# Two-layer hybrid decoder trunk: three merge columns' retention and GLA parts placed between the S5 gate blocks

## Chip, cores and metric

The kernel runs on one core of one Trainium2 chip. The metric is the device time of one execution in microseconds; the median of three runs is 2176.14 us (2175.97 to 2176.38).

## The reference

A sequence of 272 tokens (16 meta tokens and 256 others) of width 2048 passes through two layers, each a single mixer with a residual. On the same normalised input three token mixers run side by side: retention with 8 heads, gated linear attention (GLA) with 4 heads, and a diagonal complex state space model (S5) of 64 groups. Their outputs are merged column by column under sigmoid gates.

```python
h = rmsnorm(h_res, norm_g)
proj = h @ w_in
(rq, rk, rv, rg, gq, gk, gv, gg, glr, su, sg, mg) = jnp.split(proj, offs, axis=-1)
...
ro = (ro * jax.nn.silu(rg.astype(f32))).astype(dt)
...
go = (go.reshape(bsz, length, BRANCH_WIDTH) * jax.nn.silu(gg.astype(f32))).astype(dt)
...
so = jax.nn.gelu(so)
so = so * jax.nn.sigmoid(so @ s5_w_glu.astype(f32))
so = (so * jax.nn.silu(sg.astype(f32))).astype(dt)
g_r, g_g, g_s = jnp.split(mg, N_BRANCH, axis=-1)
y = (jax.nn.sigmoid(g_r) * (ro @ w_br_ret)
     + jax.nn.sigmoid(g_g) * (go @ w_br_gla)
     + jax.nn.sigmoid(g_s) * (so @ w_br_s5))
return h_res + y @ w_out
```

After the second layer a last RMSNorm follows and the meta tokens are dropped. All is float32.

## The kernel before

Activations lie transposed: 128 channels on the partitions, the 272 tokens along the free axis (256 of them in most of layer 1, where `c0` is 16). The unit of work is a block (`block`, line 180): 128 output columns of one weight matrix. It takes the weights in half blocks of eight 128x128 pieces. `prefetch` (line 128) loads each half block from memory through SyncE's queue, splits it into a rounded high part on ScalarE (ACT, line 137) and the remainder on VectorE (DVE, line 139), with three buffers for each. PE multiplies high by high, high by low and low by high. Where twice the token count fits 512 columns (layer 1, for the blocks called with `wide`), the two products with the high weights are one matmul of 512 columns (line 191), joined afterwards by a copy on ACT and an addition on DVE (lines 201 and 202); otherwise there are three matmuls a piece (lines 194 to 196).

`schedule` (line 66) is the order of all blocks of a layer, and the weights lie in memory in that order (`layout`). In order: GLA heads 0 and 1, eight S5 input blocks `su`, GLA heads 2 and 3, eight retention heads (`rv`, `rk`, `rq`, `rg`), eight S5 gate blocks `sg`, eight blocks `glu`, sixteen merge columns, sixteen output blocks. A merge column is six blocks: a sigmoid gate from the input and a projection of a branch's result, for retention (`mr`, `br`), GLA (`mgg`, `bg`) and S5 (`ms`, `bs`). The gate blocks have two half blocks, the projections one.

The S5 recurrence is a scan over 136 pairs of tokens (`s5_scan`, line 538), three instructions on GpSimd (POOL) for a step, all on the one tile `H`. It begins after the last `su` block and runs on POOL beside the GLA and retention heads. When it has ended, `s5_out(b)` (line 551) computes the eight S5 outputs: on PE one matmul of line 554, which does not read `H`, and eight of line 557, which do; on DVE nine short instructions (lines 561 to 569); on ACT a GELU. `so_split` then makes high and low parts for `glu`, which reads all eight outputs in each of its blocks.

Small pieces of work that depend on a block are put off by `after(n, fn)` (line 148): `fn` is emitted when `n` more half blocks have been emitted. `bg_finish(scan)` emits the rest of the scan. Before, it and the outputs hang on retention gate block 6:

```python
                if i == RH - 2:
                    after(6, partial(bg_finish, scan))
                    for b in range(NB):
                        after(6 + 3 * b // 2, partial(s5_out, b))
```

So output 0 follows the last block of `rq` of head 7, with that head's gate block and the eight `sg` blocks behind it. A scheduler then fixes each engine's order of instructions ahead of the run, and each engine works through its own in that order. Work tiles of 128x288 come from a pool of 17 (`U`), small PSUM tiles from a pool of five (`PT`), blocks' accumulators from three.

Of the kernel before, what the change touches and what calls it, by code (L numbers as in the profile page):

```python
# [17 lines left out]
ALU = mybir.AluOpType  # L18
# [13 lines left out]
NB = BW // P  # L32
RH = 8
# [2 lines left out]
GROUPS = 64  # L36
PAIRS = 32
HALF = T // 2

OFF = {}  # L40
_o = 0
# [24 lines left out]
def schedule():  # L66

    o = []

    def gla(h):  # L70
        o.extend([("gv", 2 * h, 16), ("gv", 2 * h + 1, 16), ("gk", h, 16), ("gq", h, 16), ("gg", 2 * h, 16),
                  ("gg", 2 * h + 1, 16)])

    gla(0)
    gla(1)
    o.extend(("su", b, 16) for b in range(NB))
    gla(2)
    gla(3)
    for h in range(RH):
        o.extend([("rv", h, 16), ("rk", h, 16), ("rq", h, 16), ("rg", h, 16)])  # L80
    o.extend(("sg", b, 16) for b in range(NB))
    o.extend(("glu", b, 8) for b in range(NB))
    for d in range(KT):
        o.extend([("mr", d, 16), ("br", d, 8), ("mgg", d, 16), ("bg", d, 8), ("ms", d, 16), ("bs", d, 8)])
    o.extend(("out", d, 16) for d in range(KT))
    return o

# [2 lines left out]
def hybrid(ctx: ExitStack, tc: tile.TileContext, xT, wst, wg, small, bcp, cst, rot, dec, out):  # L90
# [53 lines left out]
    bg = deque()  # L144
# [183 lines left out]
    for l in range(DEPTH):  # L328
# [432 lines left out]
            return h  # L761

        mg = {}
        for kind, i, nk in schedule():
            if kind == "gv":
                if i == 0:
                    after(3, partial(gla_tables, 0))
                if i % 2 == 0:
                    gl = {}
                vt = ev_v(block(x, nk, 0))  # L770
                after(1, partial(tokens, vt, False, gl, f"v{i % 2}"))
            elif kind == "gk":
                ev_gk(block(x, nk, 0), i, gl)
            elif kind == "gq":
                ev_gq(block(x, nk, c0), i, gl)
                after(1, partial(gla_scores, i, gl))
                after(3, partial(gla_apply, gl))
                after(5, partial(gla_norm, gl))
            elif kind == "gg":
                z = gate(block(x, nk, c0))  # L780
                after(7 - 3 * (i % 2), partial(lambda z, gl, i: gated(z, gl["n"][i % 2], s1, i), z, gl, i))
                if i % 2 == 0 and i < 6:
                    gla_tables(i // 2 + 1)
            elif kind == "su":
                if i == 0:
                    bg_finish(prep)
                    s5["H"] = tp.tile([P, 2, PAIRS, HALF], F32, tag="big", name=nm("H"))
                ps = block(x, nk, 0)
                V.tensor_tensor(out=su[:, i], in0=ps.rearrange("p (n e) -> p e n", e=2),  # L789
                                in1=R.rearrange("p (n e) -> p e n", e=2), op=ALU.mult)  # L790
                u2 = U().rearrange("p (a b) -> p a b", a=2)
                for v_ in range(2):
                    for pr in range(2):
                        for e in range(2):
                            G.dma_start(out=u2[64 * pr + 32 * e:64 * pr + 32 * e + 32, v_, :],  # L795
                                        in_=su[64 * v_ + 32 * pr:64 * v_ + 32 * pr + 32, i, e, :])
                after(2, partial(s5_weights, i))
                after(5, partial(s5_in, i, u2))
                if i == NB - 1:
                    scan = s5_scan()  # L800
                    after(6, partial(bg.append, scan))
            elif kind == "rv":
                if i == 0:
                    s2 = tp.tile([P, 2, NB, T], F32R, tag="s2", name=nm("ro"))
                    rot_tables()
                rl = {}
                vt = ev_v(block(x, nk, 0))
                after(1, partial(tokens, vt, True, rl, "v"))
            elif kind == "rk":
                rl["k"] = rope(block(x, nk, 0), 0)  # L810
            elif kind == "rq":
                rl["q"] = rope(block(x, nk, c0), c0)
                after(1, partial(ret_scores, i, rl))
                after(3, partial(ret_apply, rl))
                after(5, partial(ret_norm, i, rl))
            elif kind == "rg":
                z = gate(block(x, nk, c0))
                after(5, partial(lambda z, rl, i: gated(z, rl["n"], s2, i), z, rl, i))
                if i == RH - 2:
                    after(6, partial(bg_finish, scan))  # L820
                    for b in range(NB):
                        after(6 + 3 * b // 2, partial(s5_out, b))
            elif kind == "sg":
                if i == 0:
                    sgs = []
                ps = block(x, nk, c0, True)
                z = U()
                V.tensor_tensor(out=z[:, c0:], in0=ps, in1=R[:, c0:], op=ALU.mult)  # L828
                S.activation(z[:, c0:], z[:, c0:], AF.Silu)
                sgs.append(z)  # L830
                if i == 4:
                    s5["so"] = tp.tile([P, 2, NB, T], F32R, tag="big", name=nm("sohl"))
                if i >= 4:
                    for b in (2 * i - 8, 2 * i - 7):
                        so_split(b)
                        so = su[:, b, :, n0:]
                        G.tensor_tensor(out=so, in0=so, in1=sgs[b][:, c0:].rearrange("p (n e) -> p e n", e=2),
                                        op=ALU.mult)
            elif kind == "glu":
                if i == 0:  # L840
                    s3 = tp.tile([P, 2, NB, T], F32R, tag="s3", name=nm("so2"))
                z = sig(block(s5["so"], nk, c0, True), False)
                t = U()
                G.tensor_tensor(out=t[:, c0:].rearrange("p (n e) -> p e n", e=2), in0=su[:, i, :, n0:],  # L844
                                in1=z[:, c0:].rearrange("p (n e) -> p e n", e=2), op=ALU.mult)
                split(s3[:, 0, i, c0:], s3[:, 1, i, c0:], t[:, c0:])
            elif kind in ("mr", "mgg", "ms"):
                if kind == "mr" and i == 0:
                    y = tp.tile([P, 2, KT, T], F32R, tag="big", name=nm("y"))
                mg["s"] = sig(block(x, nk, c0, True))  # L850
            elif kind in ("br", "bg", "bs"):
                mv = {"br": s2, "bg": s1, "bs": s3}[kind]
                ps = block(mv, nk, c0, True)
                t = mg["s"]
                V.tensor_tensor(out=t[:, c0:], in0=ps, in1=t[:, c0:], op=ALU.mult)  # L855
                if kind == "br":
                    mg["y"] = t
                elif kind == "bg":
                    G.tensor_tensor(out=t[:, c0:], in0=t[:, c0:], in1=mg["y"][:, c0:], op=ALU.add)  # L859
                    mg["y"] = t  # L860
                else:
                    V.tensor_tensor(out=t[:, c0:], in0=t[:, c0:], in1=mg["y"][:, c0:], op=ALU.add)
                    split(y[:, 0, i, c0:], y[:, 1, i, c0:], t[:, c0:])
            elif kind == "out":
                if i == 0:
                    acc = []
                    tc.keep_in_program_order(S.preload_act_table_set("natural_log_exp_and_others"))
                    hn_next = load_h(0)
                    if last:
                        hf = tp.tile([P, KT, 256], F32, tag="s1", name=nm("hf"))  # L870
                    else:
                        xn = new_x()
                        gps, gmm = rank_gate(l + 1, xn)
                hold = hn_next
                if i < KT - 1:
                    hn_next = load_h(i + 1)
                ps = block(y, nk, c0, i < KT - 1)
                if not last:
                    h = U()
                    V.tensor_tensor(out=h, in0=ps, in1=hold, op=ALU.add)  # L880
                    split(xn[:, 0, i, :], xn[:, 1, i, :], h, sm(l + 1, "ng", i))
                    accumulate(h, acc)
                    gmm(i)
                    G.dma_start(out=h1[i], in_=h)
                else:
                    h = hf[:, i, :]
                    V.tensor_tensor(out=h, in0=ps, in1=hold[:, c0:], op=ALU.add)  # L887
                    accumulate(h, acc, c0)
                    S.activation(h, h, AF.Copy, scale=sm(l, "fg", i))
# [96 lines left out]
```

## Time and profile before

| quantity | value |
|---|---|
| median of three runs | 2176.14 us |
| the profiled execution | 2176.12 us |
| its span, first to last instruction | 2174.3 us |
| PE busy, matmuls | 2101.0 us (97%) |
| DVE / ACT / POOL busy | 1445.0 / 1022.8 / 754.1 us |
| mean granted clock of PE | 0.985 |
| loads of weight half blocks | 656 of 512 KB |

Busy time is the time in which an engine works on an instruction. PE's matmuls overlap, so a busy PE is not PE at its peak. The time of the whole is set by what ends last: where PE has work all along, a shorter time can come only from places in which it rests or runs at a lower clock. The views that are read below are the page, the list of waits (which engine and line waited for which), the timeline (instructions in order of time), the groups of instructions by line, and stretches of the span with the busy time of each engine.

### The profile page before, as it was taken

Reading aid. Unit: us, or ns where it says so; the run is one execution under the profiler, and the core shown is the slowest. Engines: PE = TensorE matmul, PEld = TensorE weight load, DVE = VectorE, ACT = ScalarE, POOL = GpSimd, SP = SyncE. Lnnn points to the kernel's source line nnn. Section 1 sums busy time; section 2 is a strip of 40 time slices with the busy share of each in tenths; the row PEclk is TensorE's granted clock in tenths of the full one; section 3 lists DMA queues with packets and bytes.
Section 4 is the critical chain, followed back from the end, with each engine's and each line's share of the span. In section 5 each row is a group of like instructions: output and inputs, shape, how many; then the busy total and the mean of one; then the engine's idle time right before and its main releaser. Section 6 shows DMA issues by size and latency. Waiting matters only on the chain. (4 is left out here: it accounts for less than half of the span.)

```text
span 2174.3 us, 39777 instructions
## 1 busy us (share of the span) xinstructions
PE 2101.0 (97%) x15650; PEld 1996.6 (92%) x15650; DVE 1445.0 (66%) x2370; ACT 1022.8 (47%) x1516; POOL 754.1 (35%) x1111
## 2 busy tenths in 40 slices
PE   9999999959999999999999999999499999999997
PEld 8999999959999999999999999999488888888886
DVE  7955888858555555555668648888496666666655
ACT  6655433326434434444446554444165444444554
POOL 3164888871200000002321548888803000000022
PEclk9999999979999999999999999999799999999999
DMA  6454444423545555445664444445235555555564
GB/s 228 137 166 137 163 161 161 161 90 125 177 175 175 175 175 175 175 175 194 210 205 147 162 141 161 168 165 172 90 107 184 194 185 192 186 190 188 189 214 152
DMA packets 108412, 365.47 MB, mean 168 GB/s; under 512 B 14016, under 2 KB 21696, under 8 KB 107968
## 3 DMA queue, kind: packets, MB, share of 16 engines
q1 hardware_dynamic: 101536, 353.73, 47.4%
q0 software_dynamic: 6400, 8.92, 1.3%
q8 instruction: 123, 2.02, 0.4%
q14 instruction: 65, 0.53, 0.1%
q10 hardware_dynamic: 288, 0.27, 0.0%
HBM read 356.32 MB, written 4.33 MB: 166 GB/s over the span
## 5 line engine op out<-in xcount | busy, mean ns | idle before, releaser
L137 ACT ACTIVATE hi<-raw 128x1024 fp32r<-128x1024 f32 x656 | 694.7, 1059 | 969.6 <-PE acc L195 574.9
L139 DVE TENSOR_TENSOR lo<-raw,hi 128x1024 fp32r<-128x1024 f32 x656 | 825.9, 1259 | 426.9 <-ACT hi L137 423.3
L196 PE MATMUL acc<-x,lo 128*128 128x272 f32 (+1 forms) x3840 | 1103.9, 288 | 2.1 <-DVE lo L139 2.1
L194 PE MATMUL acc<-x,hi 128*128 128x272 f32 (+1 forms) x2944 | 857.1, 291 | 1.1 <-ACT hi L137 0.9
L195 PE MATMUL acc<-x,hi 128*128 128x272 f32 (+1 forms) x2944 | 850.1, 289 | 0.0
L196 PEld LDWEIGHTS acc<-x,lo 128*128 128x128 f32 x3840 | 725.0, 189 | 3.8 <-DVE lo L139 3.0
L194 PEld LDWEIGHTS acc<-x,hi 128*128 128x128 f32 x2944 | 556.2, 189 | 8.0 <-issue 3.9
L195 PEld LDWEIGHTS acc<-x,hi 128*128 128x128 f32 x2944 | 556.5, 189 | 0.9
L191 PE MATMUL acc<-x,hi 128*128 128x512 f32 x896 | 317.8, 395 | 1.4 <-DVE u L828 1.2
L859 POOL TENSOR_TENSOR u<-u,u 128x272 f32<-128x272 f32 (+1 forms) x32 | 24.2, 757 | 768.1 <-DVE u L855 743.7
L542 POOL TENSOR_TENSOR pr<-H,tab 128x128 f32<-128x128 f32 x270 | 208.3, 771 | 70.9 <-ACT H L536 49.9
L191 PEld LDWEIGHTS acc<-x,hi 128*128 128x128 f32 x896 | 168.9, 189 | 41.1 <-ACT su L571 1.7
L544 POOL TENSOR_TENSOR H<-H,pr 128x64 f32<-128x64 f32 x270 | 162.2, 601 | 21.2
L545 POOL TENSOR_TENSOR H<-H,pr 128x64 f32<-128x64 f32 x270 | 143.3, 531 | 21.2
L196 PE MATMUL acc<-y,lo 128*128 128x272 f32 (+1 forms) x512 | 145.7, 285 | 0.0
L196 PEld LDWEIGHTS acc<-y,lo 128*128 128x128 f32 x512 | 96.3, 188 | 0.4
L191 PE MATMUL acc<-y,hi 128*128 128x512 f32 x240 | 83.8, 393 | 0.0
L194 PE MATMUL acc<-y,hi 128*128 128x272 f32 (+1 forms) x272 | 78.4, 288 | 0.0
L195 PE MATMUL acc<-y,hi 128*128 128x272 f32 (+1 forms) x272 | 78.2, 288 | 0.0
L795 POOL DMA_DIRECT2D u<-su x128 | 63.1, 501 | 39.2 <-DVE su L789 18.5
L196 PE MATMUL acc<-so,lo 128*128 128x272 f32 (+1 forms) x256 | 72.9, 285 | 0.0
L196 PE MATMUL acc<-ro,lo 128*128 128x272 f32 (+1 forms) x256 | 72.9, 285 | 0.0
(285 smaller groups left out, 2664.8 us busy)
## 6 DMA issues: line engine op xcount, KB each, us to landing
raw<-wst SPq DMA_DIRECT2D x656, 512.0 KB, 3.3
h<-xT SPq DMA_DIRECT2D x8, 272.0 KB, 5.6
u<-su POOLq DMA_DIRECT2D x128, 17.0 KB, 2.8
u<-dec SPq DMA_DIRECT2D x16, 136.0 KB, 3.3
u<-xT POOLq DMA_DIRECT2D x16, 136.0 KB, 2.5
h<-u POOLq DMA_DIRECT2D x16, 136.0 KB, 2.4
u<-h POOLq DMA_DIRECT2D x16, 136.0 KB, 4.2
pre<-bcp SPq DMA_DIRECT2D x2, 1024.0 KB, 8.0
```

The source lines that it names most:

```text
L137: S.activation(hi, raw, AF.Copy)
L139: V.tensor_tensor(out=lo, in0=raw, in1=hi.bitcast(F32), op=ALU.subtract)
L191: PE.matmul(ps[:, 0:2 * w].rearrange("p (j t) -> p j t", j=2), hi[:, k, :], mv[:, :, kk, c0:T], start=(kk == 0), stop=False, skip_group_ch ...
L194: PE.matmul(o, hi[:, k, :], mv[:, 0, kk, c0:T], start=(kk == 0), stop=False)
L195: PE.matmul(o, hi[:, k, :], mv[:, 1, kk, c0:T], start=False, stop=False)
L196: PE.matmul(o, lo[:, k, :], mv[:, 0, kk, c0:T], start=False, stop=(kk == nk - 1), skip_group_check=both)
L542: G.tensor_tensor(out=pr, in0=H[:, :, :, n - 1].unsqueeze(1).broadcast_to([P, 2, 2, PAIRS]), in1=tab.rearrange("p (k r) q -> p k r q", k=2 ...
L544: G.tensor_tensor(out=H[:, :, :, n], in0=H[:, :, :, n], in1=pr[:, 0], op=ALU.add)
L545: G.tensor_tensor(out=H[:, :, :, n], in0=H[:, :, :, n], in1=pr[:, 1, ::-1, :], op=ALU.add)
L795: G.dma_start(out=u2[64 * pr + 32 * e:64 * pr + 32 * e + 32, v_, :], in_=su[64 * v_ + 32 * pr:64 * v_ + 32 * pr + 32, i, e, :])
L859: G.tensor_tensor(out=t[:, c0:], in0=t[:, c0:], in1=mg["y"][:, c0:], op=ALU.add)
```

## The change

The first four `sg` blocks come, then the retention and GLA parts of merge columns 0 to 2 (`mr`, `br`, `mgg`, `bg`), then the other four `sg` blocks and `glu`. In the merge stage behind `glu`, columns 0 to 2 have only their S5 part (`ms`, `bs`) left. The end of the scan and the S5 outputs hang no longer on retention gate block 6 but on `mr` of column 1, three half blocks on. The sums of the three columns are kept, each in a work tile of its own, until `bs`; their addition of the retention and GLA parts is made by DVE, the other columns' by POOL as before. The tile `y` is allocated at the first `ms`.

```diff
@@ -36,6 +36,7 @@
 GROUPS = 64
 PAIRS = 32
 HALF = T // 2
+AHEAD_D = 3
 
 OFF = {}
 _o = 0
@@ -78,10 +79,15 @@
     gla(3)
     for h in range(RH):
         o.extend([("rv", h, 16), ("rk", h, 16), ("rq", h, 16), ("rg", h, 16)])
-    o.extend(("sg", b, 16) for b in range(NB))
+    o.extend(("sg", b, 16) for b in range(4))
+    for d in range(AHEAD_D):
+        o.extend([("mr", d, 16), ("br", d, 8), ("mgg", d, 16), ("bg", d, 8)])
+    o.extend(("sg", b, 16) for b in range(4, NB))
     o.extend(("glu", b, 8) for b in range(NB))
     for d in range(KT):
-        o.extend([("mr", d, 16), ("br", d, 8), ("mgg", d, 16), ("bg", d, 8), ("ms", d, 16), ("bs", d, 8)])
+        if d >= AHEAD_D:
+            o.extend([("mr", d, 16), ("br", d, 8), ("mgg", d, 16), ("bg", d, 8)])
+        o.extend([("ms", d, 16), ("bs", d, 8)])
     o.extend(("out", d, 16) for d in range(KT))
     return o
 
@@ -761,6 +767,7 @@
             return h
 
         mg = {}
+        s3 = None
         for kind, i, nk in schedule():
             if kind == "gv":
                 if i == 0:
@@ -816,10 +823,6 @@
             elif kind == "rg":
                 z = gate(block(x, nk, c0))
                 after(5, partial(lambda z, rl, i: gated(z, rl["n"], s2, i), z, rl, i))
-                if i == RH - 2:
-                    after(6, partial(bg_finish, scan))
-                    for b in range(NB):
-                        after(6 + 3 * b // 2, partial(s5_out, b))
             elif kind == "sg":
                 if i == 0:
                     sgs = []
@@ -845,7 +848,11 @@
                                 in1=z[:, c0:].rearrange("p (n e) -> p e n", e=2), op=ALU.mult)
                 split(s3[:, 0, i, c0:], s3[:, 1, i, c0:], t[:, c0:])
             elif kind in ("mr", "mgg", "ms"):
-                if kind == "mr" and i == 0:
+                if kind == "mr" and i == AHEAD_D - 2:
+                    after(3, partial(bg_finish, scan))
+                    for b in range(NB):
+                        after(3 + 3 * b // 2, partial(s5_out, b))
+                if kind == "ms" and i == 0:
                     y = tp.tile([P, 2, KT, T], F32R, tag="big", name=nm("y"))
                 mg["s"] = sig(block(x, nk, c0, True))
             elif kind in ("br", "bg", "bs"):
@@ -854,12 +861,13 @@
                 t = mg["s"]
                 V.tensor_tensor(out=t[:, c0:], in0=ps, in1=t[:, c0:], op=ALU.mult)
                 if kind == "br":
-                    mg["y"] = t
+                    mg[i] = t
                 elif kind == "bg":
-                    G.tensor_tensor(out=t[:, c0:], in0=t[:, c0:], in1=mg["y"][:, c0:], op=ALU.add)
-                    mg["y"] = t
+                    e = V if i < AHEAD_D else G
+                    e.tensor_tensor(out=t[:, c0:], in0=t[:, c0:], in1=mg[i][:, c0:], op=ALU.add)
+                    mg[i] = t
                 else:
-                    V.tensor_tensor(out=t[:, c0:], in0=t[:, c0:], in1=mg["y"][:, c0:], op=ALU.add)
+                    V.tensor_tensor(out=t[:, c0:], in0=t[:, c0:], in1=mg.pop(i)[:, c0:], op=ALU.add)
                     split(y[:, 0, i, c0:], y[:, 1, i, c0:], t[:, c0:])
             elif kind == "out":
                 if i == 0:
```

On PE in layer 1, where output 0 stood behind the last piece of `rq` of head 7 (`acc_18788`); `yp` is the output's PSUM tile, `K` and `C` tables of the S5 part, `su` its input. Before:

```order
L194 MATMUL acc_18788<-x_11840,hi_18754 128x256
L195 MATMUL acc_18788<-x_11840,hi_18754 128x256
L196 MATMUL acc_18788<-x_11840,lo_18756 128x256
L554 MATMUL yp_18852<-su_13031,K_1035_14157 128x128
L557 MATMUL yp_18852<-H_14166,C_13901 64x129 x8
L194 MATMUL acc_18878<-x_11840,hi_18791 128x256
L195 MATMUL acc_18878<-x_11840,hi_18791 128x256
L196 MATMUL acc_18878<-x_11840,lo_18793 128x256
```

In the change the matmuls on `H` of output 0 stand behind the last piece of `br` of column 1, which reads retention's result `ro`:

```order
L197 MATMUL acc_19374<-ro_16021,hi_19326 128x512
L202 MATMUL acc_19374<-ro_16021,lo_19328 128x256
L197 MATMUL acc_19374<-ro_16021,hi_19326 128x512
L202 MATMUL acc_19374<-ro_16021,lo_19328 128x256
L197 MATMUL acc_19374<-ro_16021,hi_19326 128x512
L202 MATMUL acc_19374<-ro_16021,lo_19328 128x256
L563 MATMUL yp_19397<-H_14166,C_13901 64x129 x8
L197 MATMUL acc_19421<-x_11840,hi_19348 128x512
L202 MATMUL acc_19421<-x_11840,lo_19350 128x256
```

Between the two places are 320 matmuls of blocks, and its first matmul, on `su`, stands among the `sg` blocks. In layer 0 the same move spans 456.

On DVE in layer 1, one S5 output (lines 561 to 569) between two weight remainders `lo`. Before, output 2, beside retention head 7 (`ur` is a part of its norm):

```order
L139 TENSOR_TENSOR lo_19028<-raw_19024,hi_19026 128x1024
L561 SCALAR_TENSOR_TENSOR su_13031<-su_13031,sm_73,yp_18994 128x128
L566 SCALAR_TENSOR_TENSOR su_13031<-su_13031,sm_73,yp_18994 32x128
L569 TENSOR_TENSOR su_13031<-su_13031,yp_18994 32x128
L566 SCALAR_TENSOR_TENSOR su_13031<-su_13031,sm_73,yp_18994 32x128
L569 TENSOR_TENSOR su_13031<-su_13031,yp_18994 32x128
L566 SCALAR_TENSOR_TENSOR su_13031<-su_13031,sm_73,yp_18994 32x128
L569 TENSOR_TENSOR su_13031<-su_13031,yp_18994 32x128
L566 SCALAR_TENSOR_TENSOR su_13031<-su_13031,sm_73,yp_18994 32x128
L569 TENSOR_TENSOR su_13031<-su_13031,yp_18994 32x128
L208 TENSOR_TENSOR ur_19021<-u_19018,ur_19020 128x256
L139 TENSOR_TENSOR lo_19077<-raw_19073,hi_19075 128x1024
```

In the change, output 1 (the same lines are 567 to 575, and 139 is 145):

```order
L145 TENSOR_TENSOR lo_19468<-raw_19464,hi_19466 128x1024
L567 SCALAR_TENSOR_TENSOR su_13031<-su_13031,sm_73,yp_19444 128x128
L572 SCALAR_TENSOR_TENSOR su_13031<-su_13031,sm_73,yp_19444 32x128
L575 TENSOR_TENSOR su_13031<-su_13031,yp_19444 32x128
L572 SCALAR_TENSOR_TENSOR su_13031<-su_13031,sm_73,yp_19444 32x128
L575 TENSOR_TENSOR su_13031<-su_13031,yp_19444 32x128
L572 SCALAR_TENSOR_TENSOR su_13031<-su_13031,sm_73,yp_19444 32x128
L575 TENSOR_TENSOR su_13031<-su_13031,yp_19444 32x128
L572 SCALAR_TENSOR_TENSOR su_13031<-su_13031,sm_73,yp_19444 32x128
L575 TENSOR_TENSOR su_13031<-su_13031,yp_19444 32x128
L145 TENSOR_TENSOR lo_19497<-raw_19493,hi_19495 128x1024
L208 TENSOR_TENSOR acc_19421<-acc_19421,u_19486 128x256
```

The S5 outputs moved from the stretch of head 7 and the gate blocks to that of merge columns 1 and 2.

On DVE at the end of `glu` in layer 1 (`so` is the result of a `glu` block). Before, after the last `glu` block's part the gate of `mr`, column 0:

```order
L139 TENSOR_TENSOR lo_19840<-raw_19836,hi_19838 128x1024
L208 TENSOR_TENSOR so_1634_19555<-u_19808,so_1634_19555 128x256
L139 TENSOR_TENSOR lo_19869<-raw_19865,hi_19867 128x1024
L202 TENSOR_TENSOR acc_19813<-acc_19813,u_19858 128x256
L752 TENSOR_TENSOR u_19861<-acc_19813,R_13015 128x256
L139 TENSOR_TENSOR lo_19896<-raw_19892,hi_19894 128x1024
L202 TENSOR_TENSOR acc_19864<-acc_19864,u_19887 128x256
L855 TENSOR_TENSOR u_19861<-acc_19864,u_19861 128x256
```

In the change its successor is the gate of `ms` (line 758), and then the product of `bs` (line 862) and the sum with the kept tile (line 870):

```order
L145 TENSOR_TENSOR lo_20311<-raw_20307,hi_20309 128x1024
L214 TENSOR_TENSOR so_1664_20026<-u_20279,so_1664_20026 128x256
L145 TENSOR_TENSOR lo_20340<-raw_20336,hi_20338 128x1024
L208 TENSOR_TENSOR acc_20284<-acc_20284,u_20329 128x256
L758 TENSOR_TENSOR u_20332<-acc_20284,R_13015 128x256
L145 TENSOR_TENSOR lo_20370<-raw_20366,hi_20368 128x1024
L208 TENSOR_TENSOR acc_20335<-acc_20335,u_20358 128x256
L145 TENSOR_TENSOR lo_20392<-raw_20388,hi_20390 128x1024
L862 TENSOR_TENSOR u_20332<-acc_20335,u_20332 128x256
L870 TENSOR_TENSOR u_20332<-u_20332,u_19292 128x256
```

`mr`, `br`, `mgg` and `bg` of column 0 stood between the last `glu` block and `ms`, and stand there no more.

## Rows read from the trace of the kernel before

**Rows 1.** Profile page: busy time by engine, and PE's busy tenths in 40 slices.

```profile
PE 2101.0 (97%) x15650; PEld 1996.6 (92%) x15650; DVE 1445.0 (66%) x2370; ACT 1022.8 (47%) x1516; POOL 754.1 (35%) x1111
...
PE   9999999959999999999999999999499999999997
```

**Rows 2.** PE's waits, whole span: us in total, times, longest.

```profile
PE yp L557 <- POOL H L545: 51.0, 2, 28.3
...
PE acc L196 <- DVE lo L139: 2.1, 3, 0.9
```

**Rows 3.** PE's timeline around S5 output 0: start us, us, instruction [idle before <-releaser].

```profile
479.46 2.08 PE L557 MATMUL yp<-H,C 128*64 128x136 f32 x16 [22.76 <-POOL H L545]
...
1573.11 1.99 PE L557 MATMUL yp<-H,C 128*64 128x129 f32 x16 [28.29 <-POOL H L545]
...
1578.83 0.38 PE L554 MATMUL yp<-su,K 128*128 128x128 f32 x2
...
1580.17 0.39 PE L194 MATMUL acc<-x,hi 128*128 128x256 f32 x1
```

**Rows 4.** Stretches of PE: us, busy (matmuls), granted clock, DMA share, GB/s.

```profile
479.40:485.00 5.60, 5.54 (x32) 0.52 0.01 3
...
1573.10:1577.00 3.90, 3.89 (x25) 0.50 0.00 0
...
1625.40:1631.50 6.10, 3.95 (x14) 0.73 0.35 99
```

**Rows 5.** POOL's timeline, scan steps that remain when PE reaches S5 output 0.

```profile
455.58 1.37 POOL L542 TENSOR_TENSOR pr<-H,tab 128x128 f32<-128x128 f32 x1
...
478.03 0.51 POOL L542 TENSOR_TENSOR pr<-H,tab 128x128 f32<-128x128 f32 x1
...
1545.91 0.51 POOL L542 TENSOR_TENSOR pr<-H,tab 128x128 f32<-128x128 f32 x1
...
1571.69 0.51 POOL L542 TENSOR_TENSOR pr<-H,tab 128x128 f32<-128x128 f32 x1
```

**Rows 6.** POOL's groups, 200 to 450, then 1300 to 1540 us: count | busy.

```profile
L542 POOL TENSOR_TENSOR pr<-H,tab 128x128 f32<-128x128 f32 x113 | 89.0, 788 | 8.9
...
L542 POOL TENSOR_TENSOR pr<-H,tab 128x128 f32<-128x128 f32 x107 | 88.5, 827 | 8.4
```

**Rows 7.** Stretches, all engines: PE, weight loads, DVE, ACT, POOL, clock, DMA, GB/s.

```profile
550.00:950.00 400.00, 400.00 (x3174) 400.00 (x3173) 214.94 (x250) 165.17 (x205) 23.41 (x23) 1.00 0.50 175
...
1700.00:2050.00 350.00, 350.00 (x2006) 307.04 (x2005) 228.76 (x322) 172.23 (x264) 10.38 (x14) 1.00 0.55 189
```

**Rows 8.** DVE's groups from 1570 to 1660 us.

```profile
L139 DVE TENSOR_TENSOR lo<-raw,hi 128x1024 fp32r<-128x1024 f32 x22 | 27.4, 1247 | 12.7 <-ACT hi L137 12.5 <-ACT u L201 0.2
...
L566 DVE SCALAR_TENSOR_TENSOR su<-su,sm,yp 32x128 f32<-32x128 f32 x32 | 10.9, 340 | 0.3
L569 DVE TENSOR_TENSOR su<-su,yp 32x128 f32<-32x128 f32 x32 | 9.2, 287 | 0.5
L202 DVE TENSOR_TENSOR acc<-acc,u 128x256 f32<-128x256 f32 x12 | 5.1, 423 | 0.8 <-ACT u L201 0.7
```

**Rows 9.** PE's timeline near the end of the gate blocks, layer 1.

```profile
1626.67 0.47 PE L191 MATMUL acc<-x,hi 128*128 128x512 f32 x1 [1.25 <-DVE u L828]
...
1628.04 0.45 PE L196 MATMUL acc<-x,lo 128*128 128x256 f32 x1 [0.91 <-DVE lo L139]
```

**Rows 10.** Timeline, end of glu, layers 0 and 1: last matmul, last subtractions.

```profile
576.02 0.29 PE L196 MATMUL acc<-sohl,lo 128*128 128x272 f32 x1
...
582.48 0.44 DVE L208 TENSOR_TENSOR so<-u,so 128x272 fp32r<-128x272 f32 x1 [1.14 <-ACT so L207]
...
1666.86 0.28 PE L196 MATMUL acc<-sohl,lo 128*128 128x256 f32 x1
...
1672.64 0.42 DVE L208 TENSOR_TENSOR so<-u,so 128x256 fp32r<-128x256 f32 x1 [0.75 <-ACT so L207]
...
1675.90 0.43 DVE L208 TENSOR_TENSOR so<-u,so 128x256 fp32r<-128x256 f32 x1 [1.09 <-ACT so L207]
```

## Prediction, on record before the change was run

> **What bounds the kernel now.** The page comes first. TensorE (PE) is busy for 2101.0 of 2174.3 us, and among the forty slices its row falls to 5 and 4 at two inner places, one in each layer [rows 1]. So the whole is PE's stream of matmuls, and only what interrupts that stream can be won. PE's list of waits says what does: 51.0 us in two waits of line 557 for POOL, against 2.1 us for the next largest entry [rows 2]. The timeline shows both: before the matmuls of S5 output 0 that read the scan's tile (line 557), PE stands for 22.76 us in layer 0 and 28.29 us in layer 1 until POOL's last scan addition [rows 3]. After such a rest the granted clock is 0.52 of full for 5.6 us and 0.50 for 3.9 us, the lower of PE's two levels (1.2 of 2.4 GHz) for nearly all of it [rows 4]. POOL is not idle in these waits. It does the remaining scan steps (three instructions each, the first on line 542): 15 starts from 455.58 to 478.03, and 18 starts from 1545.91 to 1571.69 [rows 5]. The scan is simply not finished when PE's queue reaches the S5 outputs, and everything behind in that queue waits with them.
>
> The profiled execution took 2176.12 us, 0.02 under the median of the three runs, so the sum is made from 2176.1. Some 0.2% (4.4 us) is what a measurement of this kernel can tell from no change.
>
> **The change, part by part.**
>
> *The S5 outputs move back by 19 half blocks.* Between the old and the new place of output 0 stand 456 matmuls in layer 0 (152 on each of three lines) and 320 in layer 1: 48 single ones of the last retention gate and 136 pairs. Single matmuls of 272 columns run at 400/3174 = 0.126 us each, the pairs at 350/2006 = 0.1745 per matmul [rows 7]; for 256 columns I scale the first to 0.1185. The cover is 456 x 0.126 = 57.5 us in layer 0 and 48 x 0.1185 + 272 x 0.1745 = 53.2 us in layer 1; the twelve small attention matmuls between them are left out, on the safe side. All of this is independent of the scan.
>
> *The scan is slower when PE no longer rests.* While PE and VectorE (DVE) work, a scan step takes 250/113 = 2.21 us in layer 0 and 240/107 = 2.24 us in layer 1 (instances of line 542 in those stretches, [rows 6]); in the wait, with little on DVE, the starts are 25.8/17 = 1.52 us apart, the first of them still disturbed [rows 5]. So the remainder must be counted at the slow pace: 15 x 2.21 = 33.2 us against 57.5, and 18 x 2.24 = 40.3 us against 53.2. Both waits go, with margins of 24 and 13 us. The Trainium skill, "SBUF — State Buffer", section "Who interferes with whom", says why: a DVE instruction with two SBUF inputs holds the port that GpSimd reads through, exclusively, for its whole length. By that rule alone, with the weight subtraction of line 139 (1.25 us of each 2.79 us half block), POOL keeps 55% of the time, the 27.4 us of scan left in layer 1 at the undisturbed pace would need 50 us, and the wait would be gone by a margin of 3 only, which DVE's other instructions with two SBUF inputs could use up: by the rule the second rival below, by the rows the sum as it stands. What I use is the rows' 40.3. The bound above, worked out from rows: if POOL moved only while DVE is idle, 35% of the time in the merge stage (228.76 of 350 busy, [rows 7]), it would do 0.35 x 53.2 = 18.6 of the 18 x 1.52 = 27.4 us, and PE would rest for 8.8 us. Below, the wait is zero. I take zero, since the rows of 250 and 240 us are the same contention.
>
> *Gain of this part:* 22.76 + 28.29 of rest, and the slow clock behind it, 5.6 x 0.48 + 3.9 x 0.50 = 2.7 + 1.95. Together **55.7 us**.
>
> *The load on DVE after the first S5 output.* An S5 output costs DVE 4 x 340 + 4 x 287 ns and a ninth instruction that I take like the first four, 2.85 us [rows 8]. Before, all eight fell, after the rest, together with the finishing of retention head 7, and DVE was the late one at the end: PE waited 1.25 us for a gate's evacuation and 0.91 us for a weight remainder [rows 9], and the clock fell again. In the 6.1 us from 1625.4 only 14 matmuls began [rows 4], worth 14 x 0.1745 = 2.4, so 3.7 us were lost. In the change head 7 is finished before output 0, and the outputs lie two to every three half blocks. In layer 1 such three cost DVE 3 x 1.247 (line 139) + 2 x 0.42 (line 202) + 0.85 (lines 752 and 855, of line 202's size) + 0.2 (half an addition, which the change gives to DVE) + 2 x 2.85 = 11.35 us, and PE 48 x 0.1745 + 2 x 1.34 = 11.05 us (1.34 is 1580.17 less 1578.83, [rows 3]). DVE is behind by 0.3 us per three, four times: 1.2 us. After that come gate blocks, where DVE has room. In layer 0 the three take PE 72 x 0.126 + 2.7 = 11.8 us and DVE, without the two joins, about 10.6: nothing. So I take the old loss of 3.7 as gone and 1.2 as new. The bounds are 0, since hi and lo have three buffers each to absorb it, and 3.7, the old stall once more.
>
> *What costs nothing.* The six additions that go from POOL (line 859) to DVE are in the sum above; on POOL they would have stood behind the scan. ScalarE gets four table loads fewer (50 for 54) and is 47% busy [rows 1]. SyncE issues the same loads in the new order, and only one decay table changes its place among them; DMA was busy for half of that time [rows 7]. The first matmul of output 0 is issued early in layer 1 and holds one of five PSUM buffers.
>
> *Behind glu the cover shrinks.* Before, eight half blocks stood between glu block 7 and the first use of its result in `bs`, now the two of `ms`. The chain behind glu (ACT, POOL, ACT, DVE) runs at its own pace of 1675.90 - 1672.64 = 3.26 us a block, slower than PE. In layer 1 its last subtraction ended at 1676.33, 9.2 us after PE's last glu matmul at 1667.14; in layer 0 at 582.92, 6.6 us after 576.31 [rows 10]. The last of the eight operands is wanted after two half blocks and seven eighths of a third: 16 x 2.875 x 0.1745 = 8.0 us in layer 1, 24 x 2.875 x 0.126 = 8.7 us in layer 0. So layer 1 pays 9.2 - 8.0 = 1.2 us, layer 0 nothing. Bounds: 0, if the chain runs a little ahead, and 9.2 - 5.6 = 3.6 us with some 2 us of slow clock, if `bs` has to wait with its first operand for the last one.
>
> **Sum:** 2176.1 - 55.7 - 3.7 + 1.2 + 1.2 = **2119.1**, say 2119 us, 2.6% faster.
>
> **Rivals.**
>
> *DVE becomes the bound.* The S5 outputs now share DVE with merge columns, which are its heaviest stage beside the heads. For it: 11.35 against 11.05 us, where any disorder in the queue delays a weight remainder, and a delayed remainder stops PE and lowers its clock, as [rows 9] show. Against it: the excess is small, and it is preceded by an unloaded stretch. If the old stall comes back in both layers, 2119 + 2 x 3.7 = 2126.4 us.
>
> *The scan is still late in layer 1.* For it: DVE's work slows POOL (1.52 to 2.24 us a step), and the merge columns bring DVE work of their own. Against it: the 2.24 us were themselves measured beside a working DVE, with a weight subtraction in every half block. It decides from a step of 53.2/18 = 2.96 us on. At the bound, 8.8 us of rest and some 2 us of slow clock: 2130 us.
>
> *Slower: the scratch tiles run out.* Three finished column sums now stay in the 17-buffer scratch pool from the gate blocks through glu, beside up to eight S5 gates. If more than 17 were alive, each of the 12 blocks of sg 4 to 7 and glu in each layer would have to wait with its evacuation until an older block has been used up, a pace of 3.26 us [rows 10] added to PE's own: 24 x 3.26 = 78 us, and 2119 + 78 = 2197 us. It turns into a loss from 57/24 = 2.4 us per block on. For it: nothing else in the change could cost as much. Against it: eight gates, three sums and about three temporaries are 14, and in the kernel before no listed wait of PE leads to a missing buffer.
>
> **How the numbers follow.** The forecast (2114 to 2123) has 0.74: both scan waits gone and small new waits at most. DVE as the bound has 0.14, the late scan 0.08, the scratch tiles 0.04. The range of 2114 to 2129 takes in the forecast with its bounds (2116.7 without any new stall, less some 2.5 us that the rest of the small waits in [rows 2] and the table loads may give), the upper bound at `bs` (2119.1 + 4.4), the first rival and most of the second; the third is left out, and some of the tails. Over 0.2% faster are all cases but the last: 0.96. Of the last, 0.01 would end within 0.2% and 0.03 above.
>
> **What would show it.** In the changed kernel's trace PE should have no wait for POOL's scan of more than a microsecond; from the place where PE waited before, POOL's remaining steps should take some 33 us in layer 0 and 40 in layer 1; a scan step should stay at 2.2 us to its end; and the first S5 output should start 10 us or more after the last of them. The granted clock should be 1.00 through both places. A wait of PE for line 139's successor or for a gate's evacuation between the first S5 output and glu would show the first rival, a scan step of 3 us the second, idle time before evacuations all through glu the third. Before the end of the first `bs` in layer 1 a wait of about a microsecond is expected, and none in layer 0. A time above 2129, or a wait for POOL of more than a few microseconds, would make the account wrong.

## The result, and the profile after

The changed kernel took 2115.77 us (median of four runs, 2115.58 to 2115.94), the kernel before 2176.05 us beside it: a ratio of 0.9723, 95% interval 0.9706 to 0.974. That is 3.2 us under the 2119 us of the forecast and inside the range. The profiled span fell from 2174.3 to 2113.8 us, by 60.5. Of that, 52.7 us are rest of TensorE (PE; span less busy, 73.3 before and 20.6 after) and 7.8 us are busy time.

The page of the changed kernel, PE's busy time, its busy tenths and its granted clock in tenths; the two holes of [rows 1] are gone:

```profile
PE 2093.2 (99%) x15650; PEld 1990.6 (94%) x15650; DVE 1452.3 (69%) x2376; ACT 1018.6 (48%) x1512; POOL 772.3 (37%) x1105
...
PE   9999999999999999999999999999999999999997
...
PEclk9999999999999999999999999999999999999999
```

PE's waits over the span of the changed kernel (us in total, times, longest). The entry of 51.0 us of [rows 2] is missing; the largest that is left is 1.4 us:

```profile
PE tr L640 <- DVE u L670: 1.4, 2, 1.1
PE acc L202 <- DVE lo L145: 1.2, 3, 0.7
```

Line numbers are some six higher than before: the scan is lines 548 to 551, the matmuls that read it line 563, the weight subtraction line 145. The timeline of the changed kernel, first POOL's last scan addition of each layer, then PE's first matmuls of S5 output 0:

```profile
489.27 0.37 POOL L551 TENSOR_TENSOR H<-H,pr 128x64 f32<-128x64 f32 x1
...
1561.06 0.38 POOL L551 TENSOR_TENSOR H<-H,pr 128x64 f32<-128x64 f32 x1
```

```profile
516.49 1.15 PE L563 MATMUL yp<-H,C 128*64 128x136 f32 x16
...
1573.99 1.10 PE L563 MATMUL yp<-H,C 128*64 128x129 f32 x16
```

No idle time is listed at the end of PE's rows, where [rows 3] had 22.76 and 28.29 us, and the sixteen matmuls take 1.1 us where they took 2. The scan ends at 489.64 and 1561.44: it is early by 26.8 us in layer 0 and by 12.5 us in layer 1 (1573.99 less 1561.44). Stretches that begin at output 0 (us; busy of PE, weight loads, DVE, ACT, POOL; clock; DMA) show PE full and the clock at 1.00, the higher of its two levels, where [rows 4] had 0.52 and 0.50:

```profile
516.40:560.00 43.60, 43.60 (x397) 41.11 (x396) 37.32 (x85) 24.38 (x29) 0.95 (x1) 1.00 0.39 134
1573.90:1616.00 42.10, 42.10 (x320) 35.98 (x319) 39.55 (x96) 28.27 (x41) 0.00 (x1) 1.00 0.42 139
```

### The profile page after: what moved, and what is told of

Read it like the earlier page. It is cut to its first block, busy times and chain, and to the rows that moved or that the text cites. A ratio compares the mean times of both kernels' runs of the same rounds, so it can differ in the third digit from the quotient of the medians.

```text
span 2113.8 us, 39749 instructions
## 1 busy us (share of the span) xinstructions
PE 2093.2 (99%) x15650; PEld 1990.6 (94%) x15650; DVE 1452.3 (69%) x2376; ACT 1018.6 (48%) x1512; POOL 772.3 (37%) x1105
## 5 line engine op out<-in xcount | busy, mean ns | idle before, releaser
L867 POOL TENSOR_TENSOR u<-u,u 128x272 f32<-128x272 f32 (+1 forms) x26 | 19.6, 755 | 668.0 <-DVE u L862 668.0
L548 POOL TENSOR_TENSOR pr<-H,tab 128x128 f32<-128x128 f32 x270 | 214.5, 795 | 71.0 <-ACT H L542 50.0
L550 POOL TENSOR_TENSOR H<-H,pr 128x64 f32<-128x64 f32 x270 | 174.6, 647 | 21.2
L551 POOL TENSOR_TENSOR H<-H,pr 128x64 f32<-128x64 f32 x270 | 149.7, 554 | 21.2
L862 DVE TENSOR_TENSOR u<-acc,u 128x272 f32<-128x272 f32 (+1 forms) x96 | 41.6, 433 | 46.6 <-PE acc L202 39.0
```

The source lines that it names most:

```text
L548: G.tensor_tensor(out=pr, in0=H[:, :, :, n - 1].unsqueeze(1).broadcast_to([P, 2, 2, PAIRS]), in1=tab.rearrange("p (k r) q -> p k r q", k=2 ...
L550: G.tensor_tensor(out=H[:, :, :, n], in0=H[:, :, :, n], in1=pr[:, 0], op=ALU.add)
L551: G.tensor_tensor(out=H[:, :, :, n], in0=H[:, :, :, n], in1=pr[:, 1, ::-1, :], op=ALU.add)
L867: e.tensor_tensor(out=t[:, c0:], in0=t[:, c0:], in1=mg[i][:, c0:], op=ALU.add)
```

## The experiments

Theory W: the gain is the end of PE's two waits for the scan and of the slow clock behind them. Theory D: it comes from the new order itself, which spreads VectorE's (DVE's) load. Two factors were set apart: the blocks in the new order with the outputs at the old place, and the old order with a scan that ends early. The kernel before, measured beside each group of runs, took 2175.03 to 2176.15 us in the median, so a difference of under about 1 us between runs of different groups shows nothing.

**The new order, the outputs at their old place.**

```diff
+                if i == RH - 2:
+                    after(6, partial(bg_finish, scan))
+                    for b in range(NB):
+                        after(6 + 3 * b // 2, partial(s5_out, b))
...
-                if kind == "mr" and i == AHEAD_D - 2:
-                    after(3, partial(bg_finish, scan))
-                    for b in range(NB):
-                        after(3 + 3 * b // 2, partial(s5_out, b))
```

> The three columns stay ahead of glu, but the end of the scan and the S5 outputs are called for at the old place, six half blocks behind the second last retention gate. Theory W (the gain is the end of PE's two waits for POOL's scan, and the slow clock behind them): both waits come back, 22 to 23 us in the first layer and 28 to 29 us in the second, with clock around 0.5 behind them, and the time is 2170 to 2176 us. Rival D (the gain comes from the new order itself: VectorE's load before glu is spread, the additions left POOL): the waits may be there, but a good part of the 60 us stays, 2116 to 2150 us.

Measured: 2175.53 us against 2175.41, ratio 1.0001 (0.9992 to 1.0011). The rows of this kernel, PE's list of waits and its timeline in each layer:

```profile
PE yp L563 <- POOL H L551: 50.4, 2, 27.7
...
PE acc L197 <- DVE u L835: 1.2, 1, 1.2
```

```profile
480.00 2.08 PE L563 MATMUL yp<-H,C 128*64 128x136 f32 x16 [22.73 <-POOL H L551]
...
1573.52 1.99 PE L563 MATMUL yp<-H,C 128*64 128x129 f32 x16 [27.70 <-POOL H L551]
```

Both waits are back at their old size, the sixteen matmuls behind them take 2 us again, and the whole gain is lost. Moving the columns and six additions alone is worth nothing. The old stall on a gate's evacuation (1.25 us in [rows 9]) is there too, 1.2 us, in the new order of the blocks.

**The old order, a shorter scan.**

```diff
-            for n in range(1, HALF):
+            for n in range(1, 96):
```

> The kernel before, with the last 40 of the scan's 135 steps per layer left out (its states beyond step 95 are not computed); the order of the blocks is the old one. Theory W: with some 60 to 90 us of POOL's work gone, the scan is done before the outputs want it, both waits go, and the time is 2117 to 2122 us (2176.1 less 55.7, where 3.7 of the stall on VectorE in the second layer may go or stay). Rival D: without the new order little is won, above 2150 us.

Measured: 2123.36 us (2122.8 to 2124.48), ratio 0.9763 (0.9749 to 0.9778): 52.1 us under before, and 1.4 us above the expected range. PE's waits of this kernel from 1500 to 1680 us (layer 1), and a stretch that begins half a microsecond before the first of them ends, at 1573.53:

```profile
PE acc L191 <- DVE u L828: 3.1, 1, 3.1
...
PE acc L196 <- DVE lo L139: 0.6, 1, 0.6
```

```profile
1573.00:1583.00 10.00, 8.86 (x36) 7.33 (x37) 7.66 (x11) 4.85 (x8) 2.27 (x2) 0.67 0.48 157
```

No wait for POOL is left. But the stall on DVE of [rows 9], 1.25 and 0.91 us there, is now 3.11 and 0.61 us, with a mean clock of 0.67 in 10 us (up to 3.3 us more). Together these are up to 7.0 us, where the prediction read 3.7. Without the rest before it, in which DVE could work ahead, the stall is larger. DVE's rows agree with this reason: PE's rest in layer 1 of the kernel before, the stretch from there to the end of the first wait of its stall, and the same stretch with the short scan (us; busy of PE, weight loads, DVE, ACT, POOL; clock; DMA):

```profile
1544.82:1573.11 28.29, 0.00 (x0) 0.00 (x1) 4.29 (x8) 0.80 (x1) 23.94 (x56) 0.59 0.14 48
1573.11:1626.67 53.56, 52.31 (x382) 45.37 (x382) 46.56 (x119) 34.48 (x50) 2.96 (x3) 0.96 0.29 99
```

```profile
1519.85:1573.53 53.68, 50.57 (x383) 43.84 (x382) 49.43 (x125) 35.24 (x51) 2.92 (x3) 0.99 0.37 121
```

In PE's rest DVE did 8 instructions. Without the rest, it did 125 in the stretch in place of 119, 2.9 us more of DVE's work.

**The changed kernel, the same shorter scan.**

> The changed kernel with the same 40 steps per layer left out. Theory W: the scan is wholly hidden already (margins 26.8 and 12.5 us), so nothing is left to win: 2115 to 2116.5 us. Rival: if POOL's work still costs something beside its end (its port, its semaphores, late transfers), this is faster by over 2 us, below 2113.5 us.

Measured: 2115.58 us (2115.34 to 2116.1) against 2115.77 with the whole scan. Some 160 us of POOL's work in the two layers (busy time on the page 609.8 us, with the whole scan 772.3) are worth nothing in the new order:

```profile
PE 2093.5 (99%) x15650; PEld 1990.9 (94%) x15650; DVE 1434.1 (68%) x2376; ACT 1017.6 (48%) x1512; POOL 609.8 (29%) x865
```

With the two runs before, the 60 us divide: 52.1 us come with an early scan alone, the other 7.8 (2123.36 less 2115.58) when the outputs stand between the merge columns. In the profiled executions these are 4.4 us of rest and 3.1 us of PE's busy time. So theory W holds for all but an eighth, and the eighth is the stall on DVE (up to 7.0 us of it), as theory D says. That it hangs on the outputs' place and not on the blocks' order alone is suggested by the run with the outputs at the old place, which keeps the old stall; the new order with the outputs there and a short scan was not run.

**Two columns in place of three** (`AHEAD_D = 2`).

> Two columns ahead of glu in place of three, so the outputs are called for six half blocks earlier: 13 half blocks of cover, about 39 us. Theory W: the first layer's remaining steps (33 us) are still covered, the second layer's (40 to 41 us with its margin of 12.5 us against the 17 to 18 us that six half blocks are) are not: one wait of PE for POOL of 3 to 6 us in the second layer and a short slow clock behind it, 2119 to 2124 us, no wait in the first layer. Rival D: the third column matters for VectorE's load only, no wait for POOL, 2115 to 2118 us.

Measured: 2122.16 us (2121.23 to 2122.64), 6.4 above three columns. PE's timeline in layer 1, and 10 us from just before it:

```profile
1561.38 1.99 PE L563 MATMUL yp<-H,C 128*64 128x129 f32 x16 [3.97 <-POOL H L551]
```

```profile
1561.00:1571.00 10.00, 9.62 (x62) 8.18 (x63) 5.80 (x16) 2.76 (x3) 0.32 (x1) 0.74 0.15 49
```

Without its wait, output 0 would have come at 1557.41, 16.6 us earlier than with three columns; less the margin of 12.5 us that is a wait of 4.1, and 3.97 is there. The clock of 0.74 takes up to 2.6 us more, together up to 6.6 for the 6.4 measured. In layer 0 output 0 starts at 498.5, 8.7 us behind the scan's end, and waits for nothing.

**A longer scan.**

```diff
-                G.tensor_tensor(out=pr, in0=H[:, :, :, n - 1].unsqueeze(1).broadcast_to([P, 2, 2, PAIRS]),
-                                in1=tab.rearrange("p (k r) q -> p k r q", k=2), op=ALU.mult)
+                for _ in range(24 if n == 120 else 1):
+                    G.tensor_tensor(out=pr, in0=H[:, :, :, n - 1].unsqueeze(1).broadcast_to([P, 2, 2, PAIRS]),
+                                    in1=tab.rearrange("p (k r) q -> p k r q", k=2), op=ALU.mult)
```

> The changed kernel with one product of the scan (step 120, on POOL) written 24 times in place of once: 23 more instructions of 0.70 to 0.83 us, 16 to 19 us of POOL per layer. Theory W with the margins read from the trace (26.8 us in the first layer, 12.5 us in the second): no wait in the first layer, a wait of PE for POOL of 4 to 7 us in the second with 0 to 2 us of slow clock behind it, 2119.5 to 2125 us. If the margins were only seeming (the tail of the scan has other things to wait for), waits in both layers or a longer one, over 2130 us; if POOL's end were not what PE's old wait hung on, 2115 to 2116.5 us.

Measured: 2125.54 us (2124.91 to 2126.44), 9.8 above the changed kernel, a little over the range. POOL's last addition and PE's first reading matmul in layer 1:

```profile
1582.56 0.35 POOL L552 TENSOR_TENSOR H<-H,pr 128x64 f32<-128x64 f32 x1
```

```profile
1582.96 1.99 PE L564 MATMUL yp<-H,C 128*64 128x129 f32 x16 [7.28 <-POOL H L552]
```

One wait, in layer 1 only, as theory W says. The scan ends 21.5 us later; 1.7 of them are a later arrival of PE too (1575.68 without the wait, against 1573.99; an early wait for a weight remainder is longer in this execution, the slowest of the four). The other 19.8 less 12.5 make 7.3. POOL's group of the added products in layer 1 (busy, mean ns, idle before), and the stretch behind the wait:

```profile
L549 POOL TENSOR_TENSOR pr<-H,tab 128x128 f32<-128x128 f32 x24 | 20.4, 848 | 1.9
```

```profile
1582.90:1587.20 4.30, 4.24 (x23) 3.62 (x24) 2.13 (x7) 0.00 (x0) 0.01 (x1) 0.51 0.02 4
```

So a product takes 0.85 us, 0.93 with the gap before it, where the expectation took 0.70 to 0.83, and the lower clock costs 2.1 us where it took up to 2. Both terms lie just over the range, and so does the time.

**The additions back on POOL** (`e = G` in every column).

> The six additions of the moved columns go back from VectorE to POOL, all else as in the changed kernel. If the additions cost nothing on VectorE (the prediction's view) and POOL's margins are wide enough: the same time within 1 us, 2115 to 2117 us, with the scan's end 1 to 3 us later per layer. Rival (VectorE is at its bound ahead of glu in the second layer): faster by 1 to 3 us. Rival (the additions would have stood in POOL's way): a wait for POOL in the second layer, over 2118 us.

Measured: 2116.21 us (2116.02 to 2116.72), within half a microsecond of the changed kernel. The scan ends 0.1 us earlier, not later, in layer 1 (1561.31): all six additions come behind the scan's end, the first of each layer at 507.77 and 1568.82 us. Neither rival is seen.

**Four columns in place of three** (`AHEAD_D = 4`).

> Four columns ahead of glu in place of three, the outputs called for six half blocks later still. Theory W: nothing is left to cover, the same time as with three within 1.5 us, 2114.5 to 2117 us, and margins of the scan wider by 17 to 18 us. Rival (scratch tiles are held too long): PE waits for scratch tiles ahead of glu, over 2118 us.

Measured: 2115.77 us (2115.62 to 2116.26), the same. The scan ends at 1561.12, and 16.9 us more cover changes nothing. A fourth sum in the scratch pool costs nothing either.

**More work on DVE beside the outputs.** In layer 1, from the third moved column to glu, the weight subtraction is written twice; then only every third of them.

```diff
-            V.tensor_tensor(out=lo, in0=raw, in1=hi.bitcast(F32), op=ALU.subtract)
+            state["u"] = state.get("u", 0) + state.get("dup", 0)
+            for _ in range(1 + state.get("dup", 0)):
+                V.tensor_tensor(out=lo, in0=raw, in1=hi.bitcast(F32), op=ALU.subtract)
...
+            if l == 1 and kind == "mr" and i == AHEAD_D - 1:
+                state["dup"] = 1
+            if kind == "glu":
+                state["dup"] = 0
```

> In the second layer only, from the third moved column to glu, VectorE's subtraction that makes the low half of each weight chunk (1.23 us) is written twice: 14 more instructions, 17 us of VectorE beside the S5 outputs, where it was busy 46.0 of 48.0 us. If VectorE is at its bound there and what it lacks comes out of PE: PE waits of 8 to 15 us in the second layer ahead of glu, 2124 to 2131 us. If the three-deep weight tiles and the six half blocks without outputs ahead of glu take the backlog in: under 4 us more, 2116 to 2120 us.

> As the run with every weight subtraction of that stretch written twice (17 us more of VectorE, 13 us longer), but only every third of them: 4 or 5 more instructions, 5 to 6 us of VectorE. If some 4 us of backlog are taken in by the buffers and by VectorE's idle 2 of 48 us, as the difference of 17 and 13 says: 0.5 to 3 us more than the changed kernel, 2116 to 2119 us. If VectorE has no room there at all: 5 to 6 us more, 2120.5 to 2122 us. If the stall of the first run came only of its pairs of equal instructions: no difference, under 2116.3 us.

Measured: 2129.07 us (2128.69 to 2129.11) with 14 more subtractions, 13.3 above the changed kernel, and 2119.49 us (2118.76 to 2120.37) with five more, 3.7 above. The stretch from 1577 to 1625 us, of the changed kernel, with five more and with 14 more:

```profile
1577.00:1625.00 48.00, 48.00 (x344) 41.27 (x343) 46.02 (x109) 33.53 (x50) 3.79 (x5) 1.00 0.40 133
```

```profile
1577.00:1625.00 48.00, 45.52 (x328) 38.85 (x327) 46.45 (x109) 31.88 (x47) 4.63 (x4) 1.00 0.38 121
```

```profile
1577.00:1625.00 48.00, 42.71 (x297) 35.51 (x295) 46.62 (x101) 26.49 (x40) 4.63 (x4) 0.96 0.29 99
```

DVE's busy time hardly rises, since it was already 46.0 of 48 us; PE's falls. Not all of the added work fell beside the outputs. The weight subtractions from the first to the end of the last DVE instruction of the outputs, in the same three kernels (us; busy, count; clock; DMA):

```profile
1576.22:1618.93 42.71, 12.29 (x11) 1.00 0.41 137
```

```profile
1576.47:1622.60 46.13, 15.89 (x14) 1.00 0.40 127
```

```profile
1576.82:1628.99 52.17, 20.65 (x18) 0.97 0.29 99
```

Three of the five and seven of the fourteen stand there, 3.6 and 8.4 us of DVE; the others come behind the outputs. PE's rests up to there, with five more (one) and with 14 more (two):

```profile
1624.78 0.39 PE L204 MATMUL acc<-x,lo 128*128 128x256 f32 x1 [2.48 <-DVE lo L147]
```

```profile
1620.61 0.58 PE L204 MATMUL acc<-x,lo 128*128 128x256 f32 x1 [5.29 <-DVE lo L147]
...
1626.73 0.39 PE L204 MATMUL acc<-x,lo 128*128 128x256 f32 x1 [1.63 <-DVE lo L147]
```

Of 3.6 us some 1.1 are taken in; of 8.4 some 1.4 (5.29 and 1.63 off), or none, if the 1.6 us count too that PE lost to the lower clock behind the longer rest. So DVE's room beside the outputs is about 1 us: the new order stands close to DVE's bound, and the changed kernel lies just under it. Whether weight buffers or DVE's idle time hold that room was not separated. The smaller run lies between its two expectations, which both took all of its added work to fall beside the outputs.

No run was faster than the changed kernel by more than the groups differ. Every edit tried on its scan, cover and additions left the time as it was, or lost.

## Why the prediction was right, and where it was not

**Both waits go: right.** The chain of rows 3 and 5 was the cause: with the outputs back at the old place the waits return whole, with the scan cut short they vanish even in the old order. The margins were reckoned as 24 and 13 us and are 26.8 and 12.5. The last 15 and 18 steps, from 455.44 and 1519.58 to the scan's end, take 34.2 and 41.9 us for 33.2 and 40.3. Three runs confirm the margin of layer 1 by its size: 16.6 us less cover made a wait of 4.0, some 20 us more scan one of 7.3, and 17 us more cover changed nothing. The clock is 1.00 through both places, as forecast.

**The old stall on DVE, 3.7 us: gone, as reckoned, but it is worth more by itself.** The early scan in the old order shows 52.1, and the outputs' place 7.8. The prediction's 55.7 and 3.7 have nearly the same sum, 59.4; but the waits' removal alone gives back some 4 us to that stall, which the rest before it had kept small. The sum held because the change takes both away; for the waits alone 55.7 would have been 3.6 too many.

**DVE behind by 0.3 us per three half blocks, 1.2 us: this step failed.** The weight subtractions of the changed kernel, one in every three half blocks, DVE's timeline:

```profile
1586.21 1.23 DVE L145 TENSOR_TENSOR lo<-raw,hi 128x1024 fp32r<-128x1024 f32 x1 [0.22 <-ACT hi L143]
...
1597.49 1.23 DVE L145 TENSOR_TENSOR lo<-raw,hi 128x1024 fp32r<-128x1024 f32 x1
...
1608.79 1.23 DVE L145 TENSOR_TENSOR lo<-raw,hi 128x1024 fp32r<-128x1024 f32 x1 [0.38 <-ACT hi L143]
```

They stand 11.28 and 11.30 us apart. The two stretches between them (busy of PE, weight loads, DVE, ACT, POOL):

```profile
1586.21:1597.49 11.28, 11.28 (x88) 9.67 (x84) 10.90 (x26) 7.52 (x11) 0.00 (x0) 1.00 0.41 137
1597.49:1608.79 11.30, 11.30 (x88) 9.67 (x84) 10.58 (x26) 7.54 (x11) 0.00 (x0) 1.00 0.44 145
```

The pace is PE's, which is busy all through; on its own rows a block begins behind an output at 1579.28 and again at 1590.58, 11.30 us on. PE's 11.05 was 0.25 too small: the first pair behind each of the two outputs takes 0.45 us where the others take 0.35. DVE, without its one rest of 0.38 us, takes 22.2 us for the two stretches, 11.1 each, so its 11.35 was 0.25 too large. There is no deficit but room of some 0.2 us in every three half blocks. Whether a deficit of 1.2 us would have been taken in, as the lower bound of the term supposed, the runs with more subtractions leave open, since they found room of about 1 us. They do show that the first rival was near.

**The first `bs` waits 1.2 us for the last glu result: this step failed too.** PE's timeline of the changed kernel in layer 1 (the last glu matmul, the first operand pair of `bs` 0, a pair of the block after it, the last operand pair), and DVE's subtraction that makes that last operand:

```profile
1656.54 0.28 PE L202 MATMUL acc<-sohl,lo 128*128 128x256 f32 x1
...
1662.73 0.39 PE L197 MATMUL acc<-so,hi 128*128 128x512 f32 x1
...
1665.17 0.40 PE L197 MATMUL acc<-x,hi 128*128 128x512 f32 x1
...
1666.57 0.39 PE L197 MATMUL acc<-so,hi 128*128 128x512 f32 x1
```

```profile
1665.59 0.42 DVE L214 TENSOR_TENSOR so<-u,so 128x256 fp32r<-128x256 f32 x1 [1.09 <-ACT so L213]
```

The last operand is done at 1666.01. In the order that the sum assumed its pair would have come at 1665.17 and waited 0.8 us; the order of the program puts four pairs of the next block, 1.4 us, ahead of it, and it begins at 1666.57 with no wait. The chain behind glu came out as reckoned (9.2 us behind the last glu matmul, which ends at 1656.82, for 9.2); its price did not, because the prediction counted the eight operand pairs as an unbroken row.

**What was to cost nothing cost nothing.** The additions on the other engine: 0.4 us apart. The scratch tiles: a fourth kept sum makes no difference, and PE's list of waits has the same six entries with it as with three.

With both new terms at zero the prediction's own sum gives 2176.1 - 55.7 - 3.7 = 2116.7; 2115.77 was measured. The 0.9 us between them is not assigned.

## What to carry to other kernels

Price a wait by what its end lets through: taking away the rest of one engine also takes away the time in which another one caught up, so expect the next stall to be larger than the trace of before shows it. A cover is counted in the work that stands between, and one run with less cover and one with more work under it give its margin to half a microsecond. For operand waits read the order row by row; a scheduler may already have put other work into the gap.

## What the runs showed of the hardware that was not expected

The scan's slow pace is not spread over its instructions. POOL and DVE in the changed kernel, timeline around 1557 us:

```profile
1555.57 1.23 DVE L145 TENSOR_TENSOR lo<-raw,hi 128x1024 fp32r<-128x1024 f32 x1 [1.29 <-ACT hi L143]
1555.67 1.37 POOL L550 TENSOR_TENSOR H<-H,pr 128x64 f32<-128x64 f32 x1
1556.72 0.43 DVE L208 TENSOR_TENSOR acc<-acc,u 128x256 f32<-128x256 f32 x1
1557.11 0.38 POOL L551 TENSOR_TENSOR H<-H,pr 128x64 f32<-128x64 f32 x1
1557.18 0.42 DVE L758 TENSOR_TENSOR u<-acc,R 128x256 f32<-128x256 f32 x1
1557.58 0.55 POOL L548 TENSOR_TENSOR pr<-H,tab 128x128 f32<-128x128 f32 x1
1558.21 0.36 POOL L550 TENSOR_TENSOR H<-H,pr 128x64 f32<-128x64 f32 x1
1558.32 1.32 DVE L145 TENSOR_TENSOR lo<-raw,hi 128x1024 fp32r<-128x1024 f32 x1 [0.72 <-ACT hi L143]
1558.65 1.24 POOL L551 TENSOR_TENSOR H<-H,pr 128x64 f32<-128x64 f32 x1
```

An addition of the scan takes 0.36 to 0.38 us, and the one that meets line 145 takes 1.37 or 1.24 us: it ends a quarter of a microsecond behind that subtraction, and the rows of DVE with an operand in PSUM (lines 208 and 758) do not lengthen it. The products of line 548 are held too. Of the 54 instructions of layer 1's last 18 steps 14 take over 0.8 us, each beside one of the 15 subtractions there; so one instruction per half block is held, for about a microsecond. This agrees with the rule that the prediction cited, the Trainium skill, "SBUF — State Buffer", "Who interferes with whom". As a price of the whole stage the prediction's reckoning from the rule alone was too high, though: 50 us for layer 1's remaining steps where the scan took 41.9, a margin of 3 where 12.5 was measured.

A short rest of PE did not always cost clock. With five more subtractions PE rests for 2.48 us up to 1624.78, and the stretch behind that rest shows 1.00:

```profile
1624.70:1629.00 4.30, 4.10 (x22) 3.29 (x23) 4.27 (x8) 2.93 (x5) 1.21 (x1) 1.00 0.40 122
```

Behind 3.11 and 0.61 us in the early scan of the old order it was 0.67 over 10 us, and behind 3.97 us with two columns 0.74. Nor did a longer rest always cost more: behind the 5.29 us with 14 more subtractions PE ran at the lower level for 3.2 us and then at the higher one, 1.6 us lost against up to 3.3:

```profile
1620.60:1623.80 3.20, 3.19 (x10) 2.81 (x11) 3.20 (x5) 0.42 (x1) 3.19 (x4) 0.50 0.49 164
1623.80:1629.80 6.00, 4.34 (x23) 3.29 (x22) 5.87 (x14) 3.06 (x5) 0.00 (x0) 1.00 0.26 87
```

The price of a short rest can so differ by several microseconds, and not in the order of its length. What decides it was not tried.
